# Gate and up products of four feature chunks with the weights moving, and the features turned on chip

## The chip, the cores and the metric

The kernel runs on one core of one Trainium2 chip. The metric is the device time of one execution in microseconds (us). Before the change it was 853.98 us (median of 3 runs, 853.68 to 854.66).

## What is computed

One layer of a hybrid decoder trunk in float32, for 512 tokens of width 1024: feed-forward, mixer, feed-forward.

```python
x = x + 0.5 * rms_norm(swiglu(rms_norm(x, ffn1_pre_g), ffn1_w_gu, ffn1_w_down), ffn1_post_g)
y = hybrid_mixer(rms_norm(x, mix_pre_g), ...)       # RG-LRU channels || sliding-window attention
x = x + rms_norm(y, mix_post_g)
x = x + 0.5 * rms_norm(swiglu(rms_norm(x, ffn2_pre_g), ffn2_w_gu, ffn2_w_down), ffn2_post_g)
# swiglu(x, w_gu, w_down): gate, up = split(x @ w_gu); (silu(gate) * up) @ w_down, with 2816 hidden features
```

In the mixer, the output of the recurrence is multiplied by gelu of a gate, `gate_lru`, and enters the product with `w_o` beside the attention output.

## The kernel before, in words

**Three matmuls for one product.** Every float32 operand is split into a rounded high part and a low part (the rest), and each product is three matmuls: high by high, high by low, low by high. ScalarE rounds (the `whi` casts), VectorE subtracts (the `wlo` tiles, L220 and L256). `W`, a plan of weight units, hands out a split pair of 128x1024 elements at each `W.take`, and splits up to four units ahead of the one in use (`AHEAD`, six buffers each for high and low). So VectorE and ScalarE work ahead of TensorE by up to some takes. The whole order on each engine is written out by hand: an instruction is put into its engine's queue where the Python code calls it, or, with `W.later(n, ...)`, at the n-th take from there.

**Feed-forward.** The hidden features are 22 chunks of 128. Some chunks at both ends are worked classically. For the rest, gate and up of 2 chunks are taken together as a 2x2 block product (gate or up by halves of the 1024 inner width, with two halves of the tokens), which needs seven products in place of eight (Winograd's form): `quad` (L832). One of its seven forms is 24 matmuls with 256 moving columns: a 128x128 block of the weights is stationary, 256 tokens (one token half) move, L845. Results of the two token halves lie in banks A, D and B as [feature, token].  ScalarE copies banks between forms (L867 to L884), VectorE joins them into the activated block.

Two quads, 4 chunks, make the four blocks a11, a21, a12, a22 (two chunk pairs by two token halves) for the down product, again in seven forms (`seven_down`, L946; VectorE makes the sums s1 to s4, L814 to L826). Its matmuls have 512 moving columns: a 128x128 block of the activations is stationary, the weights move (`by_tokens`, L1193 to L1195). Each finished bank is copied to a `stage` tile by ScalarE (L961) and added to partial sums in HBM by an accumulating DMA of 256 KB that GpSimd issues (L964), 14 for each group of 4 chunks. Layer 1 has three such groups (chunks 4 to 16), layer 2 has four (2 to 18). In the first group of layer 2 the classic down product of chunks 0 and 1 and the last input sums are done inside the first quad (`early`).

**Buffers.** Tiles of 128x512 come from two rings: `t2k` with 45 buffers, and `wt` with 8. Raw weights come over SyncE's queue into 5 buffers of 1 MB.

**Mixer, its end.** While TensorE does the attention products, VectorE and ScalarE make gelu of the gate for four channel chunks (`gelu_a` to `gelu_d`, L1455 to L1469). The gate is then multiplied into the recurrence on GpSimd (L1617) and, for chunks 2 and 3, on VectorE (L1614), squared, split (`ylh`, `yll`), and the norm's factors follow in `balance` (L1639: `post_eps`). The last token block's `w_o` product needs a bank that `balance` holds until `post_eps` is made.

Of the kernel before, what the change touches and what calls it, by code (L numbers as in the profile page):

```python
# [29 lines left out]
NT2K = 45  # L30
# [4 lines left out]
SEVEN_DOWN1, SEVEN_DOWN2 = (4, 16), (2, 18)  # L35
# [86 lines left out]
def tile_layer(ctx: ExitStack, tc: tile.TileContext, out: bass.AP, **ins: bass.AP):  # L122
# [16 lines left out]

    def bank(name):  # L140
        return psum.tile([P, T], F32, tag="bank", name=name)
# [53 lines left out]
    def add_quad(w_gu, f, name, early=None):  # L195


        half = slice(0, D // 2), slice(D // 2, D)
        srcs = [[w_gu[0, ks, o + f * P:o + (f + 2) * P] for o in (0, F)] for ks in half]
        rx, ry = (W.raw(lambda i=i: load_raw(srcs[i], 4, 4 * P, f"{name}{'xy'[i]}{f}_")) for i in range(2))  # L200
        gate, up = slice(0, 2 * P), slice(2 * P, 4 * P)
        a, c, b, d = (rx, gate), (rx, up), (ry, gate), (ry, up)
# [4 lines left out]
        split = ""  # L207

        def unit(block, n, after="", mid=None, post=None):
            def cast(raw):  # L210
                assert ry < W.loaded and after in split
                hi, lo = w_tiles(4, 2 * P, f"{name}{n}{f}_")
                act.copy(hi, of(block))
                return hi, lo
# [15 lines left out]
        unit(a, "p", mid=combine(dve.tensor_sub, c, a, c))  # L230
        if early:
            early()
        unit(c, "q", "p", post=combine(dve.tensor_sub, c, d, c))
        unit(c, "r", "q", mid=combine(dve.tensor_add, a, c, a))
        unit(b, "s")
        unit(a, "t", "r", mid=combine(dve.tensor_sub, b, b, c))
        unit(d, "u")
        unit(b, "v", "t")
# [37 lines left out]

    def add_down(wd, name, f, n, dh):

        r = W.raw(lambda: load_raw([wd[0, f * P:(f + n) * P, dh * T:(dh + 1) * T]], n, T, f"{name}d{f}{dh}"))
        for i in range(0, n, 2):  # L280
            add_unit(r, lambda raw, i=i: raw[:, i:i + 2, :], 2, T, f"{name}d{f + i}{dh}")
# [4 lines left out]
    def add_layer(w_gu, wd, name, groups, classic, seven, done):  # L286

        for f0, f1 in groups:
            for f in range(max(f0, done), f1, 2):
                if f < classic:  # L290
                    add_gate_up(w_gu, f, name)
                    continue
                add_quad(w_gu, f, name, f == 2 and (lambda: [add_down(wd, name, 0, 2, dh) for dh in range(2)]))
            if f1 == 2:
                continue
            if seven[0] <= f0 < seven[1]:
                add_seven_down(wd, f0, name)
            elif f1 < FC:
                for dh in range(2):
                    for f in range(f0, f1, 4):  # L300
                        add_down(wd, name, f, min(4, f1 - f), dh)
            else:
                for f, n, dh in last_order(f0, f1):
                    add_down(wd, name, f, n, dh)
# [3 lines left out]
    GROUPS1 = [(0, 4), (4, 8), (8, 12), (12, 16), (16, 22)]  # L308
    add_layer(w1, ins["ffn1_w_down"], "a", GROUPS1, CLASSIC1, SEVEN_DOWN1, 2)
# [33 lines left out]
    GROUPS2 = [(0, 2), (2, 6), (6, 10), (10, 14), (14, 18), (18, 22)]  # L343
    add_layer(w2, ins["ffn2_w_down"], "b", GROUPS2, 2, SEVEN_DOWN2, 0)

# [89 lines left out]
    def k_high(ws, banks, xs, sl, ks):  # L435


        for k in ks:
            xh = xs[k][0][:, sl]
            for (hi, lo), ps in zip(ws, banks):  # L440
                for w in (hi, lo):
                    pe.matmul(ps[:, sl], w[:, k, :], xh, start=False, stop=False, skip_group_check=True)  # L442

    def k_low(ws, banks, xs, sl):
        n = len(xs)
        for (hi, lo), ps in zip(ws, banks):
            for k in range(n):
                pe.matmul(ps[:, sl], hi[:, k, :], xs[k][1][:, sl], start=False, stop=k == n - 1, skip_group_check=True)
# [49 lines left out]
    class Next:  # L498
# [10 lines left out]
        def spread(self):  # L509
            if self.R is None:  # L510
                self.R = big.tile([P, T], F32, tag="R", name=f"R_{self.name}")
                for h in range(2):
                    act.copy(self.R[:, HALF[h]], self.rms[h].spread())

        def sums(self, k):
# [7 lines left out]
            for x, c in ((xa, k), (xb, k + 4)):  # L523
                dve.scalar_tensor_tensor(x, xT[c], self.gain(c), self.R, op0=ALU.mult, op1=ALU.mult)
# [21 lines left out]
    class Turned:  # L546


        def __init__(self, name, pre, forms=False):
            self.name, self.pre, self.t, self.made = name, pre, {}, {}  # L550
            self.xs = x_parts(name)
            self.xg = [t2k(f"xg_{name}{c}") for c in range(KD)] if forms else None

        def high(self, c, h, src):
            x_high(self.xs[c], src, col(self.pre, c), HALF[h])

        def low(self, c, h, src):
            x_low(self.xs[c], src, col(self.pre, c), HALF[h])

        def keep(self, c, h, src):  # L560
            o = self.xg[c][:, HALF[h]]
            if h:
                act.activation(o, src, AF.Copy, scale=col(self.pre, c))
            else:
                pool.tensor_add(o, *(x.bitcast(F32)[:, HALF[h]] for x in self.xs[c]))
# [45 lines left out]
    class Rows:  # L611
# [68 lines left out]
    def boundary(rows, produce, parts, turns, fills, ahead, name, beside=None):  # L680
# [37 lines left out]
        xs, (l, r) = nxt.xs, HALF  # L718
# [1070 lines left out]
```

## Time and profile before

| | before |
|---|---|
| median of 3 runs | 853.98 us |
| profiled execution | 854.44 us |
| its span, first to last instruction | 852.7 us |
| TensorE matmul (PE) busy | 840.4 us, 5667 matmuls |
| VectorE (DVE) busy | 691.5 us |
| ScalarE (ACT) busy | 549.3 us |
| GpSimd (POOL) busy | 174.6 us |
| granted TensorE clock, mean | 0.995 |

The profiled execution is 1.7 us longer than its span, and 0.46 us above the median. A busy matmul in the profile includes its way through the pipeline, and neighbours overlap, so the price of one in a stream is the distance from start to start. A row of the views ends in the time that the engine idled before it, with the one that ended the wait.

### The profile page before, as it was taken

How to read it: one execution, taken by the hardware profiler on the slowest of the kernel's cores; microseconds unless marked ns; L12 is line 12 of the kernel's file. 1: busy time of each engine (PE TensorE's matmuls, PEld its weight loads, DVE VectorE, ACT ScalarE, POOL GpSimd, SP SyncE). 2: the span in 40 equal slices, each digit the busy share in tenths (PEclk: the TensorE clock that was granted, in tenths of full speed). 3: DMA queues.
4: the chain of work that ended last, by engine and by line, in shares of the span. 5: the costliest groups of instructions: out<-in, count | busy, mean ns of one | idle time of the engine just before them, and what ended most of it. 6: DMA issues, size and time to landing. Idle time of an engine off the chain costs nothing. (4 is left out here: it accounts for less than half of the span.)

```text
span 852.7 us, 14558 instructions
## 1 busy us (share of the span) xinstructions
PE 840.4 (99%) x5667; PEld 771.8 (91%) x5667; DVE 691.5 (81%) x929; ACT 549.3 (64%) x927; POOL 174.6 (20%) x207
## 2 busy tenths in 40 slices
PE   8999999999999999999999899999999999999996
PEld 8988999999989998998778789899998998998995
DVE  4988988898897866777888677899889789789856
ACT  6647667566576555658756767767666657558552
POOL 2022005014025021015203121210502303203502
PEclk9999999999999999999999999999999999999998
DMA  8265329739549554113051454464964936938922
GB/s 248 100 198 196 123 88 247 179 94 249 161 99 255 179 173 149 50 50 100 3 110 52 144 187 145 177 177 123 242 177 105 242 124 153 219 99 197 261 87 99
DMA packets 96169, 129.17 MB, mean 151 GB/s; under 512 B 6312, under 2 KB 63972, under 8 KB 96100
## 3 DMA queue, kind: packets, MB, share of 16 engines
q1 hardware_dynamic: 76372, 86.68, 32.9%
q0 software_dynamic: 19584, 41.43, 21.9%
q8 instruction: 44, 0.72, 0.4%
q14 instruction: 25, 0.20, 0.1%
q10 hardware_dynamic: 144, 0.13, 0.0%
HBM read 93.10 MB, written 34.08 MB: 149 GB/s over the span
## 5 line engine op out<-in xcount | busy, mean ns | idle before, releaser
L964 POOL DMA_DIRECT2D yp_b<-stage x56 | 49.3, 1143 | 187.3 <-ACT stage L961 168.7
L964 POOL DMA_DIRECT2D yp_a<-stage x42 | 37.0, 1171 | 145.5 <-ACT stage L961 135.8
L1183 PE MATMUL yal<-whi_ad,hha 128*128 128x512 f32 x48 | 18.9, 393 | 0.0
L1185 PE MATMUL yal<-whi_ad,hla 128*128 128x512 f32 x48 | 18.7, 390 | 0.0
L1184 PE MATMUL yal<-wlo_ad,hha 128*128 128x512 f32 x48 | 18.7, 389 | 0.0
L880 DVE TENSOR_TENSOR u2b<-u2b,db 128x512 f32<-128x512 f32 x10 | 6.9, 686 | 12.5 <-PE db L845 12.5
L880 DVE TENSOR_TENSOR u2a<-u2a,da 128x512 f32<-128x512 f32 x9 | 6.2, 687 | 12.5 <-PE da L845 12.5
L1328 POOL TENSOR_TENSOR xcl<-xc,xch 128x512 fp32r<-128x512 f32 x4 | 5.1, 1296 | 52.3 <-ACT xch L1327 52.3
L177 DVE TENSOR_TENSOR wlo_ad<-raw_ad,whi_ad 128x1024 fp32r<-128x1024 f32 x10 | 12.2, 1220 | 4.0 <-ACT whi_ad L172 4.0
L1416 POOL TENSOR_SCALAR_AFFINE_SELECT pc<-pa 128x384 f32<-128x384 f32 x8 | 6.3, 795 | 44.2 <-ACT pa L1415 44.2
L1665 PE MATMUL wo<-whi_wo,yah 128*128 128x512 f32 x32 | 12.8, 399 | 2.4 <-DVE post_eps L1639 2.4
L177 DVE TENSOR_TENSOR wlo_wo<-raw_wo,whi_wo 128x1024 fp32r<-128x1024 f32 x8 | 11.3, 1436 | 4.6 <-ACT whi_wo L172 4.6
L624 ACT ACTIVATE sqxr<-x_rows 128x512 f32<-128x512 f32 x16 | 10.0, 630 | 5.6 <-DVE x_rows L654 5.6
L873 ACT COPY u2b<-ab 128x512 f32<-128x512 f32 x10 | 5.9, 588 | 11.9 <-PE ab L845 11.9
L1748 POOL TENSOR_TENSOR yp_b<-yp_b,grow 128x512 f32<-128x512 f32 x6 | 7.8, 1293 | 27.1 <-ACT ysq L1741 27.0
L1741 ACT ACTIVATE ysq<-yp_b 128x512 f32<-128x512 f32 (+1 forms) x9 | 5.2, 583 | 12.4 <-DVE yp_b L1740 11.7
L422 PE MATMUL gt<-xh_mx,whi_gt 128*128 128x512 f32 x32 | 13.2, 412 | 0.0
L1184 PE MATMUL ybl<-wlo_bd,hhb 128*128 128x512 f32 (+1 forms) x36 | 13.2, 366 | 0.0
L1183 PE MATMUL ybl<-whi_bd,hhb 128*128 128x512 f32 (+1 forms) x36 | 13.2, 366 | 0.0
L1185 PE MATMUL ybl<-whi_bd,hlb 128*128 128x512 f32 (+1 forms) x36 | 13.2, 365 | 0.0
L422 PE MATMUL pq<-xh_mx,whi_q 128*128 128x512 f32 x32 | 13.0, 407 | 0.0
L1665 PE MATMUL wo<-wlo_wo,ylh 128*128 128x512 f32 x32 | 12.6, 393 | 0.1
(1989 smaller groups left out, 3833.7 us busy)
## 6 DMA issues: line engine op xcount, KB each, us to landing
yp_b<-stage POOLq DMA_DIRECT2D x64, 256.0 KB, 8.5
yp_a<-stage POOLq DMA_DIRECT2D x50, 256.0 KB, 7.4
raw_ad<-in_ffn_w_down SPq DMA_DIRECT2D x4, 1024.0 KB
xn<-in_x SPq DMA_DIRECT2D x8, 256.0 KB, 3.4
x_rows<-in_x POOLq DMA_DIRECT2D x4, 512.0 KB, 12.9
yp_a<-yp_a POOLq DMA_DIRECT2D x8, 256.0 KB, 8.8
raw_q<-in_w_in SPq DMA_DIRECT2D x4, 512.0 KB, 4.0
raw_wo<-in_w_o SPq DMA_DIRECT2D x4, 512.0 KB, 7.2
```

The lines of the kernel that those rows point to most:

```text
L177: low.tensor_sub(two(lo, x), x, two(hi.bitcast(F32), x))
L422: pe.matmul(ps, hi[:, k, :], xh, start=start, stop=False)
L624: act.activation(wt(f"sq{name}{self.name}{tb}{dh}"), src, AF.Square, accum_out=self.ss[name, tb][:, dh:dh + 1])
L873: act.copy(u2, A)
L880: dve.tensor_add(u2, u2, D)
L964: pool.dma_start(o, st.rearrange("p (a b) -> p a b", a=2) if len(o.shape) == 3 else st, accum_op=ALU.add)
L1183: pe.matmul(ps, hh[:, blk], hi[:, k, cs], start=start, stop=False)
L1184: pe.matmul(ps, hh[:, blk], lo[:, k, cs], start=False, stop=False)
L1185: pe.matmul(ps, hl_[:, blk], hi[:, k, cs], start=False, stop=stop)
L1416: pool.affine_select(v4(pc)[:, 1:, :], v4(pa)[:, 1:, :], pattern=[[0, NB - 1], [1, P]], base=0, channel_multiplier=-1, compare_op=ALU.is_g ...
L1665: pe.matmul(wo_banks[tb][dh], x, w[:, k, :], start=start and k == 0 and w is hi and not xp, stop=stop and k == 1 and xp == 1, skip_group_c ...
L1748: pool.tensor_mul(y, y, grow[dh][:, c0:c1])
```

## The change

**Gate and up of 4 chunks at once** (`octo`). For the middle chunks, two quads are replaced by one block of seven forms in which the input (128 tokens of a block) is stationary and the weights move, 512 columns for 4 chunks. Banks A, D and B are now two banks each and hold [token, feature]. The input sums stay, but the tokens are dealt out differently to the two halves: each block of 128 tokens is spread as 32-token pieces (`dealt`), so that some copies, transposes and the boundary's products run over 32- or 64-element pieces.

**Turning.** The down product needs [feature, token]. VectorE turns 32x32 squares (`dve.transpose`, four of 128x512 for each octo) into a tile `squares` (`oct`, one buffer). Then `place` moves the squares into the four blocks: 32 DMAs from SBUF to SBUF of 64 rows of 512 bytes, half of them issued by SyncE and half by GpSimd.

**One group late.** The down product of a group now runs after the octo of the next group (after one quad for the last group), and its sums and splits are spread over the takes of that octo (`SevenDown.ahead`). The `stage` tiles come from the ring of 8 and no longer from that of 45, which shrinks to 41.

**Mixer.** `gelu_b(1)` and `gelu_c(1)` (VectorE and the tanh on ScalarE) stand earlier; GpSimd's four gate products run in the order 0, 2, 3, 1.

```diff
-NT2K = 45
+NT2K = 41
...
+    def dealt(t):
+        return t.rearrange("p (b i t) -> p i b t", b=NB, i=NB)
+    def natural(t):
+        return t.rearrange("p (i b t) -> p i b t", b=NB, i=NB)
+    def in_blocks(half):
+        return half.rearrange("p (i b t) -> p i b t", b=NB, i=2)
...
+    def add_octo(w_gu, f, name, early=None):
+        srcs = [[w_gu[0, k * P:(k + 2) * P, o + f * P:o + (f + 4) * P] for o in (0, F)] for k in range(0, KD, 2)]
+        order = (0, 1) if early else (0, 1, 2, 3)
+        rs = {i: W.raw(lambda i=i: load_raw(srcs[i], 2, 8 * P, f"{name}{i}{f}_")) for i in order}
+        late = [early()] if early else []
+        rs |= {i: W.raw(lambda i=i: load_raw(srcs[i], 2, 8 * P, f"{name}{i}{f}_")) for i in range(4) if i not in rs}
+        gate, up = slice(0, T), slice(T, 2 * T)
+        halves = [seven_units(((rs[i], gate), (rs[i], up), (rs[i + 2], gate), (rs[i + 2], up)), rs[i], (2, T), f"{name}{f}{i}_") for i in range(2)]
+        for n in "pqrstuv":
+            for units in halves:
+                units[n]()
+            if n == "p":
+                for add in late:
+                    add()
...
+    def add_layer(w_gu, wd, name, classic, octo, done):
+        groups = list(range(*octo, 4))
+        for f in range(done, classic, 2):
+            add_gate_up(w_gu, f, name)
+        if classic == octo[0] and classic == CLASSIC1:
+            for dh in range(2):
+                add_down(wd, name, 0, classic, dh)
+        for f in groups:
+            add_octo(w_gu, f, name, f < CLASSIC1 and (lambda: add_downs(wd, name, 0, 2)))
+            if f > groups[0]:
+                add_seven_down(wd, f - 4, name)
+        for f in range(octo[1], FC, 2):
+            add_quad(w_gu, f, name)
+            if f == octo[1]:
+                add_seven_down(wd, groups[-1], name)
+        for f, n, dh in last_order(octo[1], FC):
+            add_down(wd, name, f, n, dh)
...
+                self.dealt = big.tile([P, T], F32, tag="Rd", name=f"Rd_{self.name}")
                 for h in range(2):
-                    act.copy(self.R[:, HALF[h]], self.rms[h].spread())
+                    ps = self.rms[h].spread()
+                    act.copy(dealt(self.dealt)[:, 2 * h:2 * h + 2], in_blocks(ps))
+                    act.copy(self.R[:, HALF[h]], ps)
...
+        def half(self, t, h):
+            return t.rearrange("p (b i t) -> p b i t", b=NB, i=2)[:, :, h] if self.dealt else t[:, HALF[h]]
+        def rows(self, src):
+            return src.rearrange("p (b t) -> p b t", b=NB) if self.dealt else src
...
-                o = (2 * (c % 2) + i) * P
-                pe.transpose(self.tp[h, c - c % 2][:, o:o + P], self.xn[tb, c // 4][:, (c % 4) * P:(c % 4 + 1) * P], ident)
+                o = self.tp[h, c - c % 2][:, HALF[c % 2]]
+                o = o.rearrange("p (b i t) -> p i b t", b=NB, i=2)[:, i] if self.nxt.dealt else o[:, i * P:(i + 1) * P]
+                pe.transpose(o, self.xn[tb, c // 4][:, (c % 4) * P:(c % 4 + 1) * P], ident)
...
+        def octo(self, f, early=None):
+            n = f"{self.name}{f}"
+            nxt = self.nxt
+            aheads = iter((1, 1, 2, 2, 2, 2, 2, 2, 3, 3, 3, 3, 3, 3)) if early else iter([AHEAD] * 14)
+            def seven(banks, form, first):
+                for i in range(2):
+                    hi, lo = W.take(next(aheads), not early)
+                    for m, o in enumerate(banks):
+                        ts = slice(m * P, (m + 1) * P)
+                        for k in range(2):
+                            xh, xl = (x[:, ts] for x in nxt.t[form, 2 * i + k])
+                            for j, (x, w) in enumerate(((xh, hi), (xl, hi), (xh, lo))):
+                                pe.matmul(o, x, w[:, k, :], start=first and i + k + j == 0, stop=i == 1 and k == 1 and j == 2, skip_group_check=True)
+            def taken(name, banks):
+                ts = [wt(f"{name}{n}{m}") for m in range(2)]
+                for t, b in zip(ts, banks):
+                    act.copy(t, b)
+                return ts
+            def each(fn, *lists):
+                for xs in zip(*lists):
+                    fn(*xs)
+            def turn(h, xs):
+                for m, x in enumerate(xs):
+                    dve.transpose(squares[:, :, 2 * h + m, :], x.rearrange("p (j t) -> p j t", t=32))
+            A, D, B = ([bank(f"{s}{n}{m}") for m in range(2)] for s in "adb")
+            seven(A, "b11", True)
+            if early:
+                early()
+                for b in B:
+                    pe.matmul(b, nxt.xs[0][0][:, :P], nxt.xs[0][0], start=True, stop=True)
+            each(act.copy, B, A)
+            seven(D, "t3", True)
+            p7 = taken("p7", D)
+            seven(A, "t2", False)
+            u2 = taken("u2", A)
+            seven(B, "b21", False)
+            p1 = [wt(f"p1{n}{m}") for m in range(2)]
+            W.later(1, each, lambda o, b: act.activation(o, b, AF.Silu), p1, B)
+            seven(A, "t1", False)
+            u4 = taken("u4", A)
+            W.later(1, each, lambda o, x: dve.tensor_add(o, x, o), u4, p7)
+            seven(D, "t4", False)
+            each(lambda o, d: dve.tensor_add(o, o, d), u2, D)
+            each(lambda o, x: dve.tensor_mul(o, x, o), u2, p1)
+            squares = big.tile([P, 16, NB, 32], F32, tag="oct", name=f"sq{n}", bufs=1)
+            W.later(1, turn, 0, u2)
+            seven(A, "b22", False)
+            g1 = [wt(f"g1{n}{m}") for m in range(2)]
+            each(lambda o, b: act.activation(o, b, AF.Silu), g1, A)
+            W.later(1, each, lambda o, x: dve.tensor_mul(o, o, x), g1, u4)
+            W.later(1, turn, 1, g1)
+            self.squares = n, squares
+        def place(self, step):
+            (n, squares), (pair, h) = self.squares, divmod(step, 2)
+            block = t2k(f"h{n}{h}{pair}")
+            if step == 0:
+                self.blocks = {}
+            self.blocks[f"a{h + 1}{pair + 1}"] = block
+            for q in range(4):
+                for i in range(2):
+                    rows = slice(32 * (2 * h + i), 32 * (2 * h + i + 1))
+                    o = block[32 * q:32 * q + 32].rearrange("f (c i t) -> f i c t", c=2, i=2)[:, i]
+                    (sync if i else pool).dma_start(o, squares[rows, 8 * pair + q:8 * pair + q + 5:4].rearrange("f c b t -> f c (b t)"))
...
+        def run(self, one, part, rest):
+            n, forms = self.n, self.forms
+            A, B, Dd = ([bank(f"y{k}{n}{i}") for i in range(2)] for k in "abd")
+            rest = iter(rest)
+            for name, form, blocks in (("a", "a11", []), ("d", "s3", [(1, 1)]), ("b", "a12", [(0, 0)]), ("a", "s2", [(1, 0)]),
+                                       ("e", "s4", [(0, 1)]), ("d", "a22", [(1, 0)]), ("a", "s1", [(1, 1), (0, 1)])):
+                banks = {"a": A, "b": B, "d": Dd}.get(name) or [bank(f"ye{n}{i}") for i in range(2)]
+                one(banks, W.take(), forms[form], form in ("a11", "s3", "s4"))
                 if form == "a11":
-                    act.copy(B[i], A[i])
+                    for i in range(2):
+                        act.copy(B[i], A[i])
+                for step in next(rest, ()):
+                    self.step(step)
...
-                st = t2k("stage")
+                for i in range(2):
+                    st = wt("stage")
+                    act.copy(st, banks[i])
+                    for half, dh in blocks:
+                        o = part(half, dh, i)
+                        pool.dma_start(o, st, accum_op=ALU.add)
...
+    def placed(hid, first):
+        for step in range(4):
+            W.later(first + step, hid.place, step)
+    def octos(hid, f0, f1, parts, early=None):
+        part = lambda half, dh, i: parts[2 * half + i, dh]
+        order = ("a11", "+s3", "s3", "a12", "+s1", "+s2", "s2", "+s4", "s4")
+        down = None
+        for f in range(f0, f1 + 4, 4):
+            last, takes = f == f1, (1, 1, 2, 2, 3, 3, 4, 4, 5, 6) if f == f1 else (6, 6, 7, 8, 9, 9, 10, 11, 12, 13) if f == f0 + 4 else (1, 2, 3, 4, 5, 6, 7, 8, 9, 11)
+            if f > f0:
+                down = SevenDown(hid, f - 4)
+                down.ahead(zip(takes, order))
+            if last:
+                hid.quad(f1, False, AHEAD)
+            else:
+                hid.octo(f, None if f > f0 else early)
+            if f < f1:
+                placed(hid, 1 if f == f0 else 3)
+            if f > f0:
+                down.run(by_tokens, part, [["a22"], ["s1"]])
...
-             2: [(scan, 2), (gelu_d, 0)]}
+             2: [(scan, 2), (gelu_d, 0), (gelu_b, 1)]}
...
         if j < KC - 2:
             products(j + 2)
+        else:
+            gelu_c(1)
...
     W.cast(3)
     scan(3)
-    gelu_b(1)
-    gelu_c(1)
     pump(100)
...
-    for ci in (0, 2, 1, 3):
+    for ci in (0, 2, 3, 1):
```

Three places show the order. On TensorE, at the start of layer 2's group with chunks 10 to 13, the first rows of form b11 (ab10: bank A; whi_bp10, whi_b100_p: split weights; b11_f20: input block), before and now:

```order
L845 MATMUL ab10_7483<-b11_f20_6436,whi_bp10__7365 128x256 x2
L845 MATMUL ab10_7483<-b11_f20_6436,wlo_bp10__7366 128x256
L845 MATMUL ab10_7483<-b11_f21_6439,whi_bp10__7365 128x256 x2
L845 MATMUL ab10_7483<-b11_f21_6439,wlo_bp10__7366 128x256
L845 MATMUL ab10_7483<-b11_f22_6442,whi_bp10__7365 128x256 x2
```

```order
L926 MATMUL ab100_6650<-whi_b100_p_6497,b11_f20_5964 128x512 x2
L926 MATMUL ab100_6650<-wlo_b100_p_6498,b11_f20_5964 128x512
L926 MATMUL ab100_6650<-whi_b100_p_6497,b11_f21_5967 128x512 x2
L926 MATMUL ab100_6650<-wlo_b100_p_6498,b11_f21_5967 128x512
L926 MATMUL ab101_6651<-whi_b100_p_6497,b11_f20_5964 128x512 x2
```

Stationary and moving operand have changed places, and one matmul has twice the moving columns. Over the program 1,176 product matmuls fewer are issued.

On GpSimd's queue, during the down product of the group before (yp_b: partial sums in HBM; hb600 and hb610: blocks of the new group; sqb6: its squares), before and now:

```order
L964 DMA yp_b21_6011<-stage_6701 128x512
L964 DMA yp_b31_6013<-stage_6704 128x512
L964 DMA yp_b00_6006<-stage_6728 128x512
L964 DMA yp_b10_6008<-stage_6731 128x512
L964 DMA yp_b20_6010<-stage_6753 128x512
```

```order
L1086 DMA yp_b21_5634<-stage_6487 128x512
L1086 DMA yp_b31_5636<-stage_6490 128x512
L983 DMA hb600_6500<-sqb6_6391 32x2x128 x4
L1086 DMA yp_b00_5629<-stage_6521 128x512
L1086 DMA yp_b10_5631<-stage_6524 128x512
L983 DMA hb610_6532<-sqb6_6391 32x2x128 x4
```

Four small DMAs stand between pairs of accumulating ones, 16 more in the queue for each group.

On ScalarE, near the mixer's end (pa: attention weights; gq with L1466 or L1611: the tanh; whi_wo: weight casts; yah: the last attention rows), before and now:

```order
L1415 COPY pa_5159<-pt_5154 128x512
L172 CAST whi_wo_5164<-raw_wo_5024 128x1024
L1458 COPY gt_5180<-gt_5132 128x512
L1460 ACTIVATE gq_5182<-gt_5180 128x512
L172 CAST whi_wo_5184<-raw_wo_4852 128x1024
L1466 ACTIVATE gq_5038<-gq_5038 128x512
L493 ACTIVATE yah_5203<-po_5190,cols 128x512
```

```order
L1560 COPY pa_4784<-pt_4779 128x512
L1611 ACTIVATE gq_4662<-gq_4662 128x512
L182 CAST whi_wo_4790<-raw_wo_4477 128x1024
L1603 COPY gt_4806<-gt_4757 128x512
L1605 ACTIVATE gq_4808<-gt_4806 128x512
L182 CAST whi_wo_4810<-raw_wo_4402 128x1024
L527 ACTIVATE yah_4827<-po_4814,cols 128x512
```

The tanh of gate chunk 1 stood directly ahead of `yah`; now it stands four instructions earlier.

More of the change, by code (lines that the diff above doesn't have):

```diff
@@ L882, in quad @@
             W.later(1, low_parts, u2, 0)
-            seven(A, "b22", False, 3 if early else ahead)
+            seven(A, "b22", False, ahead)
             act.activation(g1, A, AF.Silu)
@@ L1714, in first_part @@
         W.later(8, n2.blocks)
-    middle_downs(hid, GROUPS2[1:-1], parts2, first_part)
-    f0, f1 = GROUPS2[-1]
+    octos(hid, *OCTO2, parts2, first_part)
+    f0, f1 = OCTO2[1], FC
     parts = read_parts("b", parts2)
-    hs = hid.chunks(f0, f1, ahead=5)
+    hs = quads(hid, f0, f1, ahead=5)
     for i in range(2):
```

252 lines of the change are left out of this document (114 added, 138 removed).

## The prediction

> **What bounds the kernel now.** I read the page's busy shares first, then the chain of work that ended last, then stretches of one group.
>
> ```profile
> span 852.7 us, 14558 instructions
> PE 840.4 (99%) x5667; PEld 771.8 (91%) x5667; DVE 691.5 (81%) x929; ACT 549.3 (64%) x927; POOL 174.6 (20%) x207
> ```
>
> TensorE is busy for 840.4 of 852.7 us, so at most 12 us are to be had by removing waits. More than that has to come from TensorE's own work. The chain of one group of layer 2 (start, length, what) shows its price:
>
> ```profile
> 664.92 2.87 PE ab L845 x24
> 667.80 2.88 PE db L845 x24
> ...
> 702.36 2.88 PE ab L845 x24
> 705.24 0.23 PE yab L1193
> ...
> 724.30 2.87 PE ab L845 x24
> ```
>
> One form of 24 matmuls with 256 moving columns takes 2.88 us, **120.0 ns a matmul**. The two quads take 705.24 − 664.92 = 40.32 us (336 matmuls), and the seven down forms 724.30 − 705.24 = 19.06 us for 84 matmuls with 512 columns, **226.9 ns each**. Nothing else stands in the chain: here the end is set by the number and the shape of the matmuls. By stretches:
>
> ```profile
> core 0: us, PE busy (x) PEld busy (x) DVE busy (x) ACT busy (x) POOL busy (x), PEclk, DMA share, GB/s
> 664.92:705.24 40.32, 40.32 (x338) 40.32 (x337) 32.53 (x33) 23.28 (x31) 5.30 (x6) 1.00 0.68 170
> 705.24:724.30 19.06, 19.06 (x86) 15.76 (x86) 18.20 (x21) 15.40 (x24) 7.03 (x8) 1.00 0.69 165
> 534.60:605.54 70.94, 70.93 (x472) 65.30 (x471) 65.62 (x76) 50.05 (x74) 15.59 (x24) 1.00 0.57 163
> ```
>
> The clock is 1.00 here, so both prices are at full clock. VectorE is busy for 32.53 + 18.20 = 50.73 of the group's 59.38 us (85%). In the first group of layer 2 (third stretch) it is busy for 65.62 of 70.94 (93%): it is the next bound, and the change adds work to it.
>
> **The matmuls.** Each pair of 256-column matmuls becomes one of 512 columns with the same three-way split and as many products. An octo is 168 matmuls × 226.9 ns = 38.12 us in place of 40.32, or 2.20 us less, and seven octos save **15.4 us**. That takes the down product's price over to the new form. In both, a 128x128 stationary block is loaded for each matmul. The first six down matmuls cost more:
>
> ```profile
> 645.69 0.40 PE L1193 MATMUL yab<-whi_bdp__7138,hha 128*128 128x512 f32 x1
> ...
> 646.86 0.39 PE L1195 MATMUL yab<-whi_bdp__7138,hla 128*128 128x512 f32 x1
> ```
>
> Five steps take 1.17 us, 234 ns each. If all octo matmuls cost that, 1,176 × (240.0 − 234) ns = 7.1 us are saved. I take 226.9, the mean over a whole down product. The bounds are 7.1 and 15.4.
>
> The Trainium skill, page "TensorE: Matmul & The Clock Gate", section "Back-to-back issue gap", gives a warm matmul N/2.4 + 2.5 ns. By it a pair would save only 2.5 ns, 2.9 us in all. The trace disagrees: 120.0 ns at 256 columns and 226.9 at 512 mean 13 ns beside the columns' share, paid once less for each pair.
>
> The early dummy product is one matmul longer, +0.23 us.
>
> **VectorE.** Per group the sums and splits stay and four transposes of 128x512 come in. No transpose is in the trace of before. The nearest rows:
>
> ```profile
> 711.52 0.68 DVE L826 SCALAR_TENSOR_TENSOR s4b<-s2b,u2b 128x512 f32<-128x512 f32 x1
> 712.13 0.68 DVE L797 TENSOR_TENSOR hls<-s1b,hhs 128x512 fp32r<-128x512 f32 x1
> L1347 DVE TENSOR_TENSOR_SCAN xc<-r,xc x4: 1211/1216/2302, 426.7 to 458.1; 128x512 f32<-128x512 f32 x4
> ```
>
> An elementwise tile of that size takes 0.61 us start to start. A scan over the same tile takes 1.22 (min/median/max in ns), and 2.30 beside a GpSimd tensor operation. So a transpose costs 0.6 to 2.3 us. I take 1.22, the undisturbed row of an operation that isn't plain elementwise; GpSimd has no tensor work in these groups. VectorE then needs 50.73 + 4.88 = 55.61 us of a group of 57.18: still under TensorE, with 1.57 us to spare (with 0.6, 4.0). The cost is 0 while that cover lasts.
>
> The Trainium skill, page "VectorE: DVE Perf Modes", section "The three transpose paths", has 311 ns for 128x128 in bf16. Four of these would be an estimated 1.24 us. No run shows it yet, and the sum would be the same.
>
> The tight place is layer 2's first group: 65.62 + 4.88 = 70.50 us of work in 70.94 − 2.20 = 68.74, 1.8 us too much. VectorE works some takes ahead, so part of it is absorbed: 0 to 1.8 us, I take **+0.6**. At 2.3 us a transpose it would be 6.1.
>
> **Placing the squares.** Sixteen DMAs join GpSimd's queue within each down product.
>
> ```profile
> 717.35 2.65 POOL L964 DMA_DIRECT2D yp_b<-stage  x3 [0.92 <-ACT stage L961]
> L608 POOL DMA_DIRECT2D b_f<-xh_f x4: 537/540/551, 552.2 to 556.0; - x4
> DMA to landing us min/median/max: 2.2/3.1/7.2
> L964 POOL DMA_DIRECT2D yp_b<-stage x56: 861/1206/2088, 595.4 to 792.1; - x56
> DMA to landing us min/median/max: 4.2/8.5/12.8
> q1 hardware_dynamic: 76372, 86.68, 32.9%
> ```
>
> An accumulating DMA holds the queue for 2.65 / 3 = 0.88 us and lands after 8.5. The SBUF to SBUF copy of L608 holds it 0.54 us and lands after 3.1. The queue gets 14 × 0.88 + 16 × 0.54 = 21.0 us of issues, in a down product of 19.06, so they run over by a few us. The last `place` is issued some 23 to 26 us after the down product's start and lands by 26 to 29. First used is it by VectorE's sum s1 on the fifth take of the next octo: that product is needed at its use some 19.06 + 4 × 2.72 = 30 us after that start (a take is half a form, 2.72 us). I take 0, by the nearer row L608, but this is the thinnest cover of the change: at 0.88 us an issue and 8.5 us to land it is 14 × 0.88 + 16 × 0.88 + 1.3 + 8.5 = 36 us, 6 us late. On SyncE's queue the other sixteen stand between two weight loads (`raw_bxd` and `raw_byd`) of the next down product. That is a whole octo away, so a delay of some us there is covered. The transfers themselves add 2048 packets; at 0.329 × 16 × 852.7 / 76372 = 59 ns each over 16 engines that is 7.5 us in a group whose engines are busy for 0.68 × 40.32 + 0.69 × 19.06 = 40.6 us. So they have room. ScalarE, busy 23.28 + 15.40 = 38.7 of 59.38 us, gets as many bank copies as before. Its `stage` copies now find 8 buffers in place of 45: the ninth of a down product waits for the DMA of the first, four forms or 10.9 us earlier, so by the longest landing 12.8 − 10.9 = 1.9 us, inside its idle third.
>
> **Layer 2's boundary.** Its 192 products and 32 transposes read or write pieces of 64 or 32 tokens instead of one run. If each of the three further pieces cost 13 ns, it is +7.5 us; I take 0, since the columns are as many.
>
> **The mixer's end.** The waits and the rows before them:
>
> ```profile
> PE wo L1665 <- DVE post_eps L1639: 2.4, 1, 2.4
> 458.06 2.30 DVE L1347 TENSOR_TENSOR_SCAN xc<-r,xc 128x512 f32<-128x512 f32 x1
> 460.29 1.71 DVE L1463 SCALAR_TENSOR_TENSOR gq<-gq,gt 128x512 f32<-128x512 f32 x1
> 462.03 0.63 ACT L1466 ACTIVATE gq<-gq 128x512 f32<-128x512 f32 x1 [3.45 <-DVE gq L1463]
> 462.57 0.67 ACT L493 ACTIVATE yah<-po,cols 128x512 fp32r<-128x512 f32 x1
> 463.83 0.75 DVE L496 SCALAR_TENSOR_TENSOR yal<-po,cols,yah 128x512 fp32r<-128x512 f32 x1 [1.83 <-issue]
> 466.23 0.69 DVE L1463 SCALAR_TENSOR_TENSOR gq<-gq,gt 128x512 f32<-128x512 f32 x1
> ```
>
> ScalarE stands idle 3.45 us for `gelu_b(1)`, with `yah` behind it; VectorE then idles 1.83 us for `yah`. With `gelu_b(1)` earlier, the scan starts up to 1.4 us later (two such steps at 0.69), `yah` need not wait, and `yal` follows near 461.7, 2.1 us earlier. TensorE's wait for `post_eps` is 2.4 us, so the gain lies between 0 and 2.4: I take **−2.0**. What then is late is GpSimd's products of chunks 2 and 3.
>
> **Sum.** 854.44 (profiled execution, its span 852.7 and 1.7 around it) − 15.4 + 0.2 + 0.6 − 2.0 = 837.8. The median of the runs is 853.98, 0.46 below that execution; I forecast **838 us**, own range 835 to 842.
>
> **The rivals.**
> *Squares late.* VectorE stands in its queue at s1 for the last `place`, and behind it the splits of the next takes. At 6 us late against 1.6 to 4 us to spare, 2 to 4.4 us per group are lost. VectorE's lead (four takes ahead of the one in use, five of 2.72 us, some 13 us) covers layer 1's three groups, not the four of layer 2, where the first group uses it up: 4 × 2 to 4 × 4.4 us, so 846 to 855. For it: the queue is over 19.06 us in any case; 12.8 us landings exist. Against: L608's 0.54 and 3.1.
>
> *Shape worth less.* At 234 ns the sum is 854.44 − 7.1 + 0.8 − 2.0 = 846.1. With the skill's page it would be near 850. Against: every down product runs at 226.9.
>
> *VectorE becomes the bound (slower side).* With 2.6 us a transpose a group needs 50.73 + 10.4 = 61.1 us, 1.75 more than the whole group before; layer 1 keeps its 6.6 by its lead, layer 2 loses 3 × 1.75 and 65.62 + 10.4 − 70.94 = 5.1 in its first group: 854.44 − 2.0 − 6.6 + 10.4 = 856. Gain and loss cancel at 2.5 us, a little above the scan's 2.30. For it: an operation with no row, writing small strided runs. Against: L826 at 0.68 in the same down product.
>
> *The order doesn't help* (mixer gain 0, boundary dear): 838 + 2 to + 9.5, so 840 to 847.5, within the range either way.
>
> **How the numbers follow.** Forecast 0.62, with 838; squares late 0.17; shape worth less (or the boundary dear) 0.09; VectorE the bound 0.12. What a measurement here can tell from no change is about 0.2%, 1.7 us. The first and the third lie under 853.98 − 1.7 = 852.3, and of the second about 0.11: faster 0.82. Another 0.04 of the second ends within 0.2%, and its last 0.02 with the fourth case above: slower 0.14. The range begins at 834: 854.0 − 15.4 − 2.4 + 0.2 = 836.4, 0.6 less if the first matmuls of an octo aren't dear as those of a down product, and 1.7 for the measurement. It ends at 849, which takes in the third case and the lower half of the second; about 0.2 is left above.
>
> **What would show it.** Octo forms at 168 × 227 ns between starts, TensorE without waits in the groups; transposes near 1.2 us; the last `place` landing before s1; `post_eps` no longer waited for. Wrong would be a matmul at 233 ns or more, waits of TensorE for split weights with VectorE held by squares, or transposes above 2 us.

## The result, and the profile after

The changed kernel takes **845.05 us** (median of 5 runs, 843.75 to 848.59), against 853.98 before: a ratio of 0.9902, 95% interval 0.9874 to 0.9931. The forecast was 838 us. So the time went the way that was forecast, by 8.9 us and not by 16; it lies inside the stated range of 834 to 849 and outside the forecast's own 835 to 842. The profiled execution took 847.83 us, in a span of 846.1. It is one of the long ones: its mean granted clock was 0.991, that of the shortest execution (843.75 us) 0.998.

The first two lines of the page, and then the chain of waits at layer 1's first octo (start, length, what):

```profile
span 846.1 us, 12674 instructions
PE 828.3 (98%) x4492; PEld 712.6 (84%) x4492; DVE 703.4 (83%) x957; ACT 547.0 (65%) x929; POOL 235.7 (28%) x319
```

```profile
82.42 5.44 PE aa L926 x24
87.86 5.44 PE da L926 x24
```

TensorE's busy time fell by 12.1 us, but its share of the span fell too, from 99% to 98%: waits have come in. An octo form is 5.44 us for 24 matmuls, 226.7 ns each, as the forecast had it (226.9). So the gain of the matmuls was there in full, 2.2 us for each octo, and something took back about 7 us. The list of TensorE's waits shows where (sum, times, longest, in us):

```profile
PE ybb L1316 <- ACT ybb L1076: 2.8, 2, 2.1
...
PE aa L867 <- ACT u4a L895: 1.3, 1, 1.3
PE g_ps L1165 <- DMA g1rows<-in_ffn_pre_g: 1.1, 1, 1.1
PE a_first L1173 <- ACT xh_a L527: 0.9, 1, 0.9
PE yba L1316 <- ACT yba L1076: 0.8, 1, 0.8
PE wo L1810 <- DVE post_eps L1784: 0.7, 1, 0.7
PE ybl L1306 <- ACT hhb L875: 0.5, 1, 0.5
PE yb L1307 <- DVE wlo_bd L187: 0.4, 1, 0.4
PE ab L867 <- ACT u4b L895: 0.4, 1, 0.4
```

`post_eps` fell from 2.4 to 0.7. New are the waits for ScalarE's copies from bank to bank: `ybb` and `yba` (L1076, bank A into bank B in a down product) and `u4` (L895, in the quad behind the last octo of a layer). They lie in three places only: layer 2's first down product, and the last quad with its down product in each layer. The 0.5 and 0.4 us for `hhb` and `wlo_bd` are new too, and they stay in every version of the changed kernel below. A steady group (octo, then down product; columns as in the stretches of before) has none:

```profile
641.00:679.00 38.00, 38.00 (x169) 31.49 (x168) 32.80 (x37) 23.86 (x32) 11.64 (x16) 1.00 0.83 200
679.00:698.00 19.00, 19.00 (x85) 15.73 (x85) 18.93 (x21) 14.68 (x23) 9.87 (x14) 1.00 0.75 175
626.09:629.50 3.41, 3.41 (x10) 2.63 (x9) 3.41 (x6) 3.41 (x6) 0.62 (x1) 0.50 0.90 287
```

The third stretch stands directly behind the longest new wait: there the granted clock was 0.50 for 3.41 us, which costs another 1.7 us.

**Layer 2's first down product.** TensorE, ScalarE and VectorE in time order, each from its own timeline:

```profile
623.22 0.39 PE L1318 MATMUL ydb<-whi_bdq__6347,hls3b 128*128 128x512 f32 x1
625.66 0.50 PE L1316 MATMUL ybb<-whi_bdr__6368,hha12b 128*128 128x512 f32 x1 [2.05 <-ACT ybb L1076]
```

```profile
624.07 1.04 ACT L280 CAST whi_bdu__6442<-raw_byd__6203 128x1024 fp32r<-128x1024 f32 x1 [5.27 <-DVE raw_byd__6203 L291]
625.02 1.06 ACT L1076 COPY ybb<-yab 128x512 f32<-128x512 f32 x2
```

```profile
618.17 1.22 DVE L284 TENSOR_TENSOR wlo_bdr__6369<-raw_byd__6203,whi_bdr__6368 128x1024 fp32r<-128x1024 f32 x1
620.44 1.30 DVE L941 STREAM_TRANSPOSE sqb<-u2b 128x512 f32<-128x512 f32 x2
622.77 1.21 DVE L291 TENSOR_TENSOR raw_byd__6203<-raw_bxd__5996,raw_byd__6203 128x1024 f32<-128x1024 f32 x1
```

The split weight that the waiting matmuls need, `wlo_bdr`, was ready at 619.39, more than 6 us before. What was missing is a bank copy, and it stood in ScalarE's queue behind the cast of a weight unit that is used three forms later. That cast waited 5.27 us for VectorE's sum. Two transposes took 1.30 us, start to start 0.61 each.

**The last quad of layer 1.** VectorE, then ScalarE:

```profile
247.81 0.69 DVE L1050 TENSOR_TENSOR s1a<-ha,ha 128x512 f32<-128x512 f32 x1 [2.96 <-DMA ha<-sqa]
```

```profile
249.32 0.62 ACT L1033 CAST hhs2a<-s2a 128x512 fp32r<-128x512 f32 x1 [3.32 <-DVE s2a L1052]
252.68 0.58 ACT L895 COPY u4a<-aa 128x512 f32<-128x512 f32 x1
```

VectorE stands at s1 for the last square. s2's cast stands on ScalarE, waiting for it, and the bank copy `u4a` behind that.

### The profile page after: what moved, and what is told of

It is laid out like the page before. It is cut to its first block, busy times and chain, and to the rows that moved or that the text cites. A ratio compares the mean times of both kernels' runs of the same rounds, so it can differ in the third digit from the quotient of the medians.

```text
span 846.1 us, 12674 instructions
## 1 busy us (share of the span) xinstructions
PE 828.3 (98%) x4492; PEld 712.6 (84%) x4492; DVE 703.4 (83%) x957; ACT 547.0 (65%) x929; POOL 235.7 (28%) x319
## 4 chain that ended last, share of the span: by engine, by line
PE 46%; issue 21%; DMA 10%; DVE 8%; POOL 7%; ACT 7%; SPq 0%; DVEq 0%; POOLq 0%; ACTq 0%
DMA yp_b<-stage 6%; DMA yp_a<-stage 4%; POOL hb L983 3%; PE aa L867 3%; PE ab L926 3%; POOL ha L983 2%; PE db L926 2%; PE aa L926 2%; PE a_first L1173 2%; POOL yp_b L1086 1%; PE ab L867 1%; PE da L867 1%; PE an L772 1%; PE yal L1306 1%; PE yal L1307 1%
## 5 line engine op out<-in xcount | busy, mean ns | idle before, releaser
L1086 POOL DMA_DIRECT2D yp_b<-stage x56 | 53.3, 1250 | 119.7 <-ACT stage L1083 115.8
L1086 POOL DMA_DIRECT2D yp_a<-stage x42 | 40.2, 1304 | 91.1 <-ACT stage L1083 83.8
L983 POOL DMA_DIRECT2D hb<-sqb x64 | 41.3, 772 | 46.0 <-PE db L926 37.7
L983 POOL DMA_DIRECT2D ha<-sqa x48 | 30.5, 774 | 49.1 <-DVE sqa L941 44.4
L926 PE MATMUL aa<-whi_a_p,b_a 128*128 128x512 f32 x48 | 14.8, 389 | 0.0
L926 PE MATMUL ab<-whi_b_p,b_f 128*128 128x512 f32 x48 | 14.8, 389 | 0.0
L825 POOL TENSOR_TENSOR usa<-usa,gsa 128x512 f32<-128x512 f32 x3 | 4.7, 1595 | 33.3 <-ACT gsa L817 29.4
L1333 POOL DMA_DIRECT2D yp_b<-stage x8 | 4.3, 540 | 31.5 <-ACT stage L1332 30.7
```

Source lines behind the costliest of these rows:

```text
L926: pe.matmul(o, x, w[:, k, :], start=first and i + k + j == 0, stop=i == 1 and k == 1 and j == 2, skip_group_check=True)
L983: (sync if i else pool).dma_start(o, squares[rows, 8 * pair + q:8 * pair + q + 5:4].rearrange("f c b t -> f c (b t)"))
L1086: pool.dma_start(o, st, accum_op=ALU.add)
```

## The experiments

All are timed in five rounds, beside runs of the kernel before on the same chip (853 to 855.6 us). Two theories for the lost 7 us were open: **coupling** (late squares in the last quads, and a thin lead in layer 2's first down product, each reaching TensorE through ScalarE's queue) and **VectorE the bound** (its added work).

### The squares not moved

```diff
-            squares = big.tile([P, 16, NB, 32], F32, tag="oct", name=f"sq{n}", bufs=1)
+            squares = {}
...
-                    dve.transpose(squares[:, :, 2 * h + m, :], x.rearrange("p (j t) -> p j t", t=32))
+                    squares[h, m] = t2k(f"h{n}{h}{m}")
+                    dve.transpose(squares[h, m].rearrange("p (j t) -> p j t", t=32), x.rearrange("p (j t) -> p j t", t=32))
...
-            for q in range(4):
-                for i in range(2):
-                    ...
-                    (sync if i else pool).dma_start(o, squares[rows, 8 * pair + q:8 * pair + q + 5:4].rearrange("f c b t -> f c (b t)"))
+            self.blocks[f"a{h + 1}{pair + 1}"] = tiles[h, pair]
```

(with `NT2K` at 45, the room that `squares` had)

> The turned squares are read where VectorE wrote them (a tile of their own each), and the 32 transfers of each octo are left out, so the blocks of the down product hold wrong features. Theory (squares late): after the change TensorE waits 1.46 + 0.91 us at layer 1's last quad and its down product, and 0.56 + 0.92 us at layer 2's, because the last squares land late. These waits go, about 3.9 us: some 841 us median against 845.05. The wait of 2.05 us in layer 2's first down product stays, as VectorE's work stays. Rival (VectorE's extra work is the cause everywhere): all waits stay, 844 to 845.

Measured: 841.51 us, ratio 0.985 (0.9837 to 0.9863). TensorE's waits:

```profile
PE ybb L1312 <- ACT ybb L1072: 2.0, 1, 2.0
```

Of the new waits for bank copies that is all that is left: the last quads and their down products are free of them, and layer 2's first down product still waits. So the transfers cost about 3.5 us, all at the last quads and the down products behind them, and the other wait has another cause.

### Each transpose twice

```diff
-                    dve.transpose(squares[:, :, 2 * h + m, :], x.rearrange("p (j t) -> p j t", t=32))
+                    for _ in range(2):
+                        dve.transpose(squares[:, :, 2 * h + m, :], x.rearrange("p (j t) -> p j t", t=32))
```

> Each transpose is made twice (same output), 4 x 0.6 = 2.4 us more on VectorE for each octo. Theory (VectorE has cover in the steady groups, 51.7 of 57 us, and none in layer 2's second octo): no TensorE waits in the steady groups, 2 to 4 us more in layer 2's first down product and up to 1 at the last quads, 847 to 850. Rival (VectorE is already the bound): 7 x 2.4 = 17 us more, about 862.

Measured: 868.63 us, ratio 1.0164 (1.015 to 1.0177), 23.6 us above the changed kernel. The theory as I had written it fails: it said 847 to 850. But the rival's price, all of VectorE's added work, 17 us, is exceeded too. The waits of TensorE and a row of ScalarE, at layer 1's first down product:

```profile
PE ybb L1317 <- ACT ybb L1077: 6.1, 3, 4.2
PE aa L867 <- ACT ba L887: 5.3, 2, 5.0
PE yba L1317 <- ACT yba L1077: 4.4, 3, 2.9
PE ab L867 <- ACT bb L887: 3.7, 1, 3.7
PE ab L926 <- DVE wlo_b_r L224: 2.0, 1, 2.0
```

```profile
162.76 1.04 ACT L280 CAST whi_adu__1648<-raw_ayd__1407 128x1024 fp32r<-128x1024 f32 x1 [6.15 <-DVE raw_ayd__1407 L291]
163.71 1.06 ACT L1077 COPY yba<-yaa 128x512 f32<-128x512 f32 x2
```

Of 21.5 us in these five lines, 2.0 are for a split weight; the rest is for bank copies on ScalarE, one of them in the row behind its cast. The longest, 5.0 us at layer 1's last quad, is for a copy `ba` behind a cast (`hha11a`, L1034) that waited 3.31 us for squares to land. Either theory may hold now, and the next two runs tell them apart.

### The bank copies ahead of the cast

```diff
-                one(banks, W.take(), forms[form], form in ("a11", "s3", "s4"))
+                one(banks, W.take(AHEAD, form != "a11"), forms[form], form in ("a11", "s3", "s4"))
```

In each down product ScalarE's cast of unit u moves from ahead of the copies L1076 to behind them. Nothing moves on TensorE or VectorE.

> One place on ScalarE's queue in each down product: the copies of bank A into bank B (L1076) come ahead of the cast of unit u, not behind it; VectorE's and TensorE's orders stay. Theory (coupling: in layer 2's first down product TensorE waited 2.05 us for the copies, which stood behind a cast that waited 5.3 us for VectorE, while the split weights were 6.6 us ahead of use): that wait and the clock slice behind it go, up to 3.7 us, and 0.75 + 0.75 us at the last down products: 840.5 to 842.5. Rival (VectorE itself is late): the wait moves to a split weight or to the next copy, 844 to 845.

Measured: 840.2 us, ratio 0.9836 (0.9823 to 0.9848). ScalarE in layer 2's first down product:

```profile
617.18 0.57 ACT L1076 COPY ybb<-yab 128x512 f32<-128x512 f32 x1 [0.79 <-PE yab L1318]
...
620.22 1.05 ACT L280 CAST whi_bdu__6464<-raw_byd__6203 128x1024 fp32r<-128x1024 f32 x1 [1.93 <-DVE raw_byd__6203 L291]
```

The copies follow their matmuls at once, the cast still waits for VectorE, and TensorE no longer waits here. That is coupling: VectorE was no faster, and 4.9 us came back.

### Each transpose twice, the bank copies first

Both edits above together.

> Each transpose twice, and the bank copies ahead of the cast. Against each transpose twice alone (868.6 us): theory (coupling) takes away the waits for L1077 copies in the down products, 3.1 + 0.9 + 0.9 + 4.4 + 1.3 + 0.9 = 11.5 us, and one or two clock slices of 1.7: 854 to 859. Rival (VectorE is the bound): no change, 866 to 869.

Measured: 849.12 us, ratio 0.9936 (0.992 to 0.9952); 19.5 us less than with the transposes alone, and more than the theory gave. VectorE's doubled turning costs 8.9 us with the copies first (849.12 − 840.2) and 23.6 us with the cast first. So most of what added VectorE work costs here is the order on ScalarE. A rest is VectorE's own, and 1.7 and 1.0 us of waits for bank copies at the last quads are left as well:

```profile
PE ab L926 <- DVE wlo_b_r L224: 2.0, 1, 2.0
...
PE ydb L1318 <- DVE wlo_bdu__6485 L284: 1.0, 1, 1.0
```

### The last octo's squares placed two takes earlier

```diff
-                placed(hid, 1 if f == f0 else 3)
+                placed(hid, 1 if f in (f0, f1 - 4) else 3)
```

> Only the last octo of each layer places its squares two takes earlier (takes 1 to 4 of the down product, not 3 to 6), 5.4 us. Theory (squares late at the last quad, since only one quad lies between): the waits of 3.9 us in all at the two last quads go, some 841. Rival (GpSimd's queue of accumulating transfers, not the take, sets when the last square lands): the landing moves by less than 2 us and TensorE still waits, 844 to 845.

Measured: 845.58 us, ratio 0.9892 (0.9879 to 0.9905): no gain. VectorE's sums no longer wait for squares (5.1 us at L1050 in the profile of the change), so the squares did land in time. But TensorE still waits at the last quads, now for the quad's first bank copy. ScalarE, and TensorE's waits:

```profile
234.49 0.59 ACT L1083 COPY stage<-yda 128x512 f32<-128x512 f32 x1 [2.73 <-DMA yp_a<-stage]
```

```profile
PE aa L867 <- ACT ba L887: 1.8, 1, 1.8
...
PE ab L867 <- ACT bb L887: 1.1, 1, 1.1
```

ScalarE's copies into `stage` now wait for accumulating transfers to land; that this is for want of buffers in the ring of eight is how I read it. That they land later because the placing goes ahead of them in GpSimd's queue is my reading too. Neither theory had this.

### The same, with stage tiles from the ring of 41

```diff
-                    st = wt("stage")
+                    st = t2k("stage")
```

> The last octo of each layer places its squares two takes earlier, and the stage tiles come from the ring of 41 again, not from that of 8. With the early places alone TensorE still waited 1.8 and 1.1 us at the last quads, behind stage copies that waited 4.3 us for the landing of accumulating transfers. Theory (the ring of 8 hands GpSimd's late queue on to ScalarE): these waits go, 841 to 842.5. Rival (the squares are still late): 844 to 845.

Measured: 878.88 us, ratio 1.0285 (1.0271 to 1.0298), 33 us worse. ScalarE:

```profile
235.72 1.07 ACT L1083 COPY stage<-yaa 128x512 f32<-128x512 f32 x2 [8.11 <-DMA yp_a<-stage]
```

From the larger ring, in which blocks, sums and split parts live too, the copies wait longer here, up to 8.1 us, not shorter. So with the early places it is worth a great deal that the change took `stage` out of that ring; the ring of 41 without the early places was not run, and why it holds the copy up was not followed further.

### The last group's sums later

```diff
-            ... (1, 1, 2, 2, 3, 3, 4, 4, 5, 6) if f == f1 ...
+            ... (1, 1, 2, 2, 4, 4, 5, 5, 6, 7) if f == f1 ...
```

The takes of the last quad at which VectorE and ScalarE prepare the last down product; from s1 on, each is one take (2.88 us) later, not the one or two that the expectation of the second run below speaks of.

> The changed kernel with the later sums of the last group alone. Theory: the waits for u4 at the last quads (1.3 and 0.4 us in the profile of the change) go, the wait of 2.05 us in layer 2's first down product and its clock slice stay, 842 to 844. Rival: no change, 844 to 845.5.

Measured: 845.93 us, ratio 0.9896 (0.9877 to 0.9916): no change.

```profile
PE ybb L1316 <- ACT ybb L1076: 3.4, 2, 2.0
PE yba L1316 <- ACT yba L1076: 1.7, 1, 1.7
PE ab L867 <- ACT u2b L891: 1.5, 1, 1.5
```

The waits for `u4` at the last quads went, and came back as 1.7 and 1.4 us for the copies L1076 of the last down products, behind the cast of unit u as elsewhere, and as 1.5 us for `u2b` at layer 2's last quad. With these copies first:

> The bank copies ahead of the cast, and in the last quad of each layer the sums and casts for the last down product (s1, s2, s4) one or two takes later, 2.9 to 5.8 us, still ahead of their use. Theory (squares late: s1 waited 3.5 us for the last square and ScalarE's bank copies stood behind what follows from s1): the last quads' waits of 0.3 and 1.8 us go, 838 to 839. Rival (the lateness passes on to the down product): a wait there, 840 to 841.

Measured: **837.85 us** (837.83 to 838.95), ratio 0.981 (0.9797 to 0.9824). The longest of TensorE's waits behind the start, and what is left of those for `u4`:

```profile
PE wo L1810 <- DVE post_eps L1784: 0.8, 1, 0.8
...
PE aa L867 <- ACT u4a L895: 0.5, 1, 0.5
```

This version beats both kernels, with the whole computation, by two edits of one line each: 7.2 us under the change, 16.4 under the 854.23 of its own runs of before.

### No transfers of squares, the bank copies first

> No transfers of squares (the blocks hold wrong features) and the bank copies ahead of the cast: the two losses taken out together. Theory (they are all that the forecast of 838 missed): 841.5 less 2.05 and a clock slice of 1.6, so 837.5 to 838.5. If the octo were dearer than 226.9 ns a matmul, or VectorE's load cost more elsewhere, it would stay above 840.

Measured: 837.07 us (836.3 to 837.9), ratio 0.9799. Slightly below the expected 837.5. What the octo itself costs is therefore no more than forecast, and in the net the two couplings are all that the forecast missed. Smaller terms may cancel in that: the 0.9 us of waits for `hhb` and `wlo_bd` stay, and the mixer gave a little more than forecast, as the next runs show.

### The mixer's order

The change's order on the kernel before (gelu_b(1), gelu_c(1) earlier; gates 0, 2, 3, 1):

> The kernel before with the mixer's gelu and gate order of the change alone. Theory: post_eps comes 1.7 us earlier, so 852.3 to 852.6 against 854.2. If the 5 us that undoing it in the changed kernel cost were all its own, 849.

Measured: 851.24 us against 854.76, ratio 0.9963 (0.995 to 0.9976), so 2.1 to 4.3 us. In its profile:

```profile
PE wo L1665 <- DVE post_eps L1639: 0.8, 1, 0.8
```

Undone in the changed kernel:

> The changed kernel with the mixer's gelu and gate order of before. Theory: the wait for post_eps goes back from 0.7 to 2.4 us and nothing else moves, +1.7 to +2.0: 846.5 to 847. Rival: the shorter wait came from elsewhere (other timing before the mixer): no change, 845.

Measured: 849.99 us, ratio 0.9951 (0.9936 to 0.9966), 4.9 us more, where 1.7 to 2.0 were expected.

```profile
PE aa L867 <- ACT u4a L895: 2.8, 1, 2.8
PE wo L1810 <- DVE post_eps L1784: 2.4, 1, 2.4
PE ybb L1316 <- ACT ybb L1076: 2.0, 1, 2.0
PE ab L867 <- ACT u2b L891: 1.8, 1, 1.8
```

The `post_eps` wait is back at 2.4, as expected, and in this execution a stretch at half clock stands behind it and behind two of the other waits. One of these two, 2.8 us for `u4a` where the changed kernel's profile has 1.3, lies in layer 1, ahead of everything that this edit touches: that wait differs from execution to execution. To see the mixer's order without the couplings, it was undone in the version of 837.85:

> The version with the bank copies ahead of the cast and the later sums, with the mixer's order of before. Theory: the wait for post_eps is 2.4 us in place of 0.75, 1.65 us, and in some executions a clock slice behind it, up to 1.7 more: 839.5 to 841.3 against 837.85. If the mixer's order were itself worth the 5 us that undoing it in the changed kernel cost: 842.8.

Measured: 842.05 us, but from 840.24 to 849.16 (ratio 0.9866, 0.9837 to 0.9896). The difference is 4.2 us, with runs too far apart to size it: the profiled execution has the 2.4 us wait with half clock behind it, and a wait of 1.9 us at layer 2's last quad that the profile of the version of 837.85 did not show.

The profiles size the order itself. From the start of the mixer's first product (`an`) to that of its last (`wo`), TensorE takes 155.85 us in the kernel before and 153.55 with the change's order, 2.3 us less. In the version of 837.85 it takes 153.54, and 156.73 with the order undone: 3.2 us more, with the half-clock stretch in it. The rest of what these profiles differ by lies outside the mixer: at the start of the program, where nothing was changed, and in layer 2. Whether the order has a part in that of layer 2 stays open.

## Why the prediction was right or wrong

*The matmuls* were right: 226.7 ns against 226.9, and 1.00 of the clock in the steady groups. The rival that a 512-column matmul is worth less fell, and with it the sum by 2.5 ns a matmul. The Trainium skill, page "TensorE: Matmul & The Clock Gate", section "Back-to-back issue gap", gives that rule for an isolated matmul; by it 512 columns take an estimated 215.8 ns. Here, where the profile counts 4492 weight loads for 4492 matmuls, they take 226.7.

*The boundary* with its strided pieces was taken at 0, and the stretch from the mixer's last block of products to layer 2's first form took 30.35 us against 30.30.

*The mixer* was right in kind and nearly in size: −2.0 forecast, 2.3 us less between its first and last product, 1.7 of it at the wait.

*VectorE's transposes* were mis-sized, and the step behind them was wrong. A transpose is 0.61 us start to start, at the low end of 0.6 to 2.3, not the 1.22 I took (nor the 1.24 estimated from the Trainium skill's page "VectorE: DVE Perf Modes", section "The three transpose paths"; here the measurement decides). The step that failed is "the cost is 0 while that cover lasts", with its 1.57 us to spare: I compared VectorE's busy time with the length of a group. Doubling the transposes gives just the 1.22 us apiece that I took, and the kernel then takes 868.6 us: by my own price the answer would have been slower than before. The rival on the slower side was put at 2.5 us a transpose; in this kernel it decides at less than 1.22. A wrong price and a wrong cover hid each other; that the term came out small was luck. What counted was not when split weights are ready (they were 6 us ahead) but that ScalarE's queue holds casts for takes ahead, some of them waiting for VectorE, in front of copies that TensorE needs now.

*The tight place in layer 2's first group* was named, with +0.6; there it cost 2.05 us of wait and, in the profiled execution, 1.7 of clock. Its way to TensorE was not the split weights but the bank copy; reordering that alone gave back 4.9 us in all.

*Placing the squares* was taken at 0, "the thinnest cover of the change". The step that failed is the time of need: I worked out 30 us from a whole octo behind the down product. Behind the last octo comes a quad, and the sums stand on its third take. From the rows

```profile
215.54 0.39 PE L1316 MATMUL yaa<-whi_adp__2060,hha11a 128*128 128x512 f32 x1
...
234.58 0.40 PE L867 MATMUL aa<-b_a,whi_a_p 128*128 128x256 f32 x2
```

the down product starts at 215.54 and the quad at 234.58, so the third take is at 234.58 + 2 × 2.88 = 240.3, 25 us after the start. The last square was there at 247.8, 32 us after it, where I had 26 to 29. And the landing was mis-sized too (L983; then the same issues' landing):

```profile
L983 POOL DMA_DIRECT2D ha<-sqa x48: 533/555/1757, 128.3 to 241.0; - x48
DMA to landing us min/median/max: 1.7/4.6/10.6
```

The issue cost what row L608 said (0.54), the landing 4.6 us in place of 3.1. So this rival was right for two groups of seven, not for the steady ones, and cost 3.5 us. The ring of eight was sized rightly: the longest wait of a `stage` copy for a landing was 2.0 us, where I had 1.9.

*The sum.* In the profiled execution, 847.83 − 837.8 = 10 us are too much: 2.05 + 1.7 in layer 2's first down product, 1.3 + 0.4 + 0.75 + 0.75 at the last quads and their down products, about 1 in small waits (`hhb`, `wlo_bd`), and at the start some 1.7 (waits for `g1rows` and `xh_a` and a longer stretch at half clock): the first octo starts at 82.3 us here, the first quad of before at 80.6, and the other profiles of the record lie between 79.3 and 80.8. Less the 0.6 that the forecast had for the low lead, that makes 9 of the 10. With the 0.3 that the mixer gave beyond the forecast, some 1.2 us are not accounted for.

## What to carry to other kernels

An engine's busy share of a stage says that it can keep up, not that it will be in time: follow the instruction that the bound engine needs next back through its in-order queue, and look for one ahead of it that waits for work not needed until later. Before a long-latency chain is shortened or an engine sped up, try moving the urgent short copy ahead of the early cast; here that gave back 4.9 of the 7 us that the change fell short. And work out the time of need for the last group apart, since what follows it is shorter than in the steady state.

## What was not expected of the hardware

Half-clock stretches follow waits much shorter than I had thought to matter. In the clock's records of these runs the stretches are 3.41 us long, or a multiple, but for the last of a run, which its end cuts off; and within one run they start on a grid of 3.41 us. I laid this grid over TensorE's busy time, from the program's first 10 us on. Where TensorE idled 2.0 us or more within one cell of the grid, the clock was 0.50 in the next cell in every case (18 cells in 7 profiles). With 1.77 and 1.81 us it was as well, with 1.85 and 1.88 not, and with 1.70 or less never, unless the cell itself was already at half clock. In the first cell of the records, 5 to 8 us from the start, less was enough: 0.53 us in one profile, while 0.66 us in another was not.

The 2.4 us wait of the kernel before fell across two cells, 1.40 and 1.01 us, and cost nothing more. So a wait near 2 us costs 2 or 3.7 us by its place on the grid. That fits the spread of the changed kernel, 4.8 us between executions of which the two longest have the lowest mean clocks (0.991 and 0.993), against 1.1 us in the version of 837.85, which has no such wait. It is not the whole of the spread: with the squares not moved, executions that differ by only 0.3 us have a wait of 2.0, and with the mixer's order undone in the version of 837.85 they differ by 8.9 us at clocks of 0.994 to 0.996. Where this comes from stays open.

The Trainium skill, page "TensorE: Matmul & The Clock Gate", section "What's actually happening", has the free-running window of 3413 ns, and the runs agree. Its advice to avoid idle gaps above about 3 us ("Why this matters for your kernels") is too lax by these numbers: about 1.8 us within one window was enough.
